# Two chunks of every feed-forward net by seven half-size products that add up in PSUM, with half-sums made by accumulating DMAs

## The chip, the cores and the metric

The kernel runs on one core of one Trainium2 chip. Times are device microseconds of one execution. The core has a matrix engine (TensorE: PE for products, PEld for its weight loads), VectorE (DVE), ScalarE (ACT), GpSimd (POOL) and SyncE (SP), which here only issues DMAs. Each engine takes its instructions in its own order; SP and POOL are also queues of DMA issues, in which an issue that has to wait holds up those behind it.

## The reference

Two layers over 256 tokens of width 1024, all in float32. Each layer is a feed-forward net, a mixer, a cross-attention to 256 memory rows and a second feed-forward net, each with a residual and a layer norm:

```python
def swiglu(x, w_gate, w_up, w_down):
    return (jax.nn.silu(x @ w_gate) * (x @ w_up)) @ w_down

for l in range(DEPTH):      # DEPTH = 2, D_MODEL = 1024, D_FF = 2816
    h = layer_norm(ALPHA * h + 0.5 * swiglu(h, ffn1_gate[l], ffn1_up[l], ffn1_down[l]), ...)
    ...                     # mixer: conv, gated recurrence, pooling; w_in, w_out
    h = layer_norm(ALPHA * h + cross_attn(h, mem, ca_q[l], ca_k[l], ca_v[l], ca_o[l]), ...)
    h = layer_norm(ALPHA * h + 0.5 * swiglu(h, ffn2_gate[l], ffn2_up[l], ffn2_down[l]), ...)
```

The four nets (`ffn1` and `ffn2` of both layers) are what the change touches, and the place of the turned memory, which `cross_attn` needs.

## The kernel before

Every float32 operand is split into two float32r parts, high and low: ACT casts the high part (L61), DVE subtracts it from the source for the low part (L62), and PE makes three products instead of one (high by high, high by low, low by high; `mm_rows`). A product of 128 x 128 by 128 x 512 is one matmul instruction (L105).

A net (`ffn`) goes over the 2816 hidden columns in chunks of 512, the last of 256. A chunk takes 2 MB of `gate` and 2 MB of `up`, in four tiles of 128 x 1024 (512 KB) each. `load` issues a tile on SP into one of 6 `raw` buffers; the split writes one of 8 `whi` and 8 `wlo` buffers, which come free when PE has used them, so ACT and DVE run at most 8 tiles ahead of PE. A plain chunk (`hidden`) is 96 matmuls: 2 token tiles x 8 rows of blocks x 3 parts x 2 matrices. Then the gated product is made on ACT (silu, L436) and DVE (L440), turned by four small DMAs and a DVE transpose (`turn`: L450, L453) and split into `ah`, `al`. `both(c, u)` takes half of a chunk through `down`: one slab of two 512 KB tiles and 24 matmuls, which add into four PSUM banks (`dn`) over the whole net. Slabs run behind the chunks: in the iteration of chunk c stand `both(c - 2, 1)` and `both(c - 1, 0)`. The last three slabs, in `end`, run row by row with the layer norm (`finish`, L332 to L358).

Some chunks go by `by_seven`: [x00 x01; x10 x11] (token halves by halves of the 1024 inputs) times [w00 w01; w10 w11] (upper and lower halves of `gate` and `up`) by seven products of 12 matmuls instead of eight, so 84 matmuls. It needs sums of blocks of x (`blocks_of_x`, made once a net from four quarters of x) and sums of weight blocks, which DVE adds in place in the raw tiles (L597): w00 + w01, then + w11, w01 + w11, then w00 + w10 by adding w10: 8 additions of 128 x 1024 per chunk. The products' results are combined on DVE (`put`, L619). Chunks 2 and 4 (the third and fifth) of three nets are done so, but in the very first net (`early` is set) chunk 4 alone: there the spare buffers hold the memory rows, which POOL loads by 32 small DMAs (L193) and DVE turns during chunk 2 (L202), and small parameters.

The order in each engine's queue is made by a scheduler from the program's dependences and its own costs; the start of the first net is written by hand (`manual_schedule` in `first`). PSUM has four `acc` banks and four `dn` banks.

Of the kernel before, what the change touches and what calls it, by code (L numbers as in the profile page):

```python
# [17 lines left out]
P = 128  # L18
# [15 lines left out]

class Weights:
# [11 lines left out]
def model(ctx: ExitStack, tc: tile.TileContext, t: dict, out: bass.AP):  # L47
# [16 lines left out]
    def load(src, k0, nk, c0, ncol, fine=False):  # L64


        hi, lo, todo = [], [], []
        step = 2048 // ncol
        for a in range(k0, k0 + nk, step):
            half = step // 2  # L70
            raw = [
                wp.tile([P, 1024], F32, tag="raw", name="raw", bufs=6).rearrange("p (k c) -> p k c", c=ncol)
                for _ in range(2)
            ]
            part = 1 if fine else half
            for b in range(0, step, part):
                loads.append(nc.sync.dma_start(
                    raw[b // half][:, b % half : b % half + part, :],
                    src[(a + b) * P : (a + b + part) * P, c0 : c0 + ncol].rearrange("(k p) c -> p k c", p=P),
                ))  # L80
# [12 lines left out]
        return Weights(hi, lo, half, todo)  # L93
# [8 lines left out]
    def product(o, w, x, start, stop):  # L102
        x = x.rearrange("p (h c) -> p c h" if len(x.shape) == 2 else "p r (h c) -> p r c h", h=2)
        o = o.rearrange("p (c h) -> p c h" if len(o.shape) == 2 else "p r (c h) -> p r c h", h=2)
        nc.tensor.matmul(o, w, x, start=start, stop=stop)  # L105
# [23 lines left out]
    def mm_rows(o, xh, xl, wh, wl, start, stop):  # L129
        product(o, xh, wh, start, False)  # L130
        product(o, xh, wl, False, False)
        product(o, xl, wh, False, stop)
# [30 lines left out]
    mT = cst.tile([P, NK, 2, SEQ], F32R, name="mT")  # L163
    xTh, xTl = xT[:, :, 0, :], xT[:, :, 1, :]
    mTh, mTl = mT[:, :, 0, :], mT[:, :, 1, :]
# [17 lines left out]
    def load_memory(mp, behind):  # L183
        m = [
            mp.tile([P, DM], F32, tag=f"spare{n}", name="m", bufs=1).rearrange("p (k b j) -> p k b j", k=4, j=32)
            for n in range(2)
# [11 lines left out]
        def later():  # L198
            for n in range(2):
                for k in range(0, 4, 2):  # L200
                    turned = mp.tile([P, 2, SEQ], F32, tag="up", name="turned")
                    nc.vector.transpose(  # L202
                        turned.rearrange("p k t -> p (k t)"), m[n][:, k : k + 2].rearrange("p k b j -> p (k b j)")
                    )
                    d = slice(4 * n + k, 4 * n + k + 2)
                    split(mTh[:, d, :], mTl[:, d, :], turned)
# [14 lines left out]
    def small_parameters(op):  # L221
        spare = op.tile([P, DM], F32, tag="spare2", name="rows", bufs=1)
# [177 lines left out]
    def ffn(l, name, n, pend=None, last=False, early=None):  # L400
        gate, up, down = (t[f"{name}_{x}"][l] for x in ("gate", "up", "down"))
        with tc.tile_pool(name="ffn", bufs=2, reuse_waits="tile") as fp:
# [24 lines left out]
            def ordered(v):  # L427
                return v.rearrange("p (a k j) -> p k a j", a=4, j=32)

            def by_two(v, o):  # L430
                o = o.rearrange("p (n a j m) -> p m n a j", n=2, a=4, m=2)
                return [(ordered(v)[:, 2 * m : 2 * m + 2], o[:, m]) for m in range(2)]

            def activate(s, i, og):
                for v, o in by_two(s[:, i, :], og):
                    nc.scalar.activation(v, o, AF.Silu)  # L436

            def gated(s, i, ou):
                for v, o in by_two(s[:, i, :], ou):
                    nc.vector.tensor_tensor(v, o, v, op=ALU.mult)  # L440
# [5 lines left out]
            def turn(s):  # L446
                ah, al = act_tiles()
                x = fp.tile([P, 4, NT, P], F32, tag="dealt", name="dealt", bufs=1)
                for a in range(4):
                    nc.sync.dma_start(x[a * 32 : a * 32 + 32], s[:, :, a * P : (a + 1) * P])  # L450
                for i in range(NT):
                    d = fp.tile([P, 4, P], F32, tag="up", name="square")
                    nc.vector.transpose(  # L453
                        d.rearrange("p k (b r) -> p b k r", b=4), x[:, :, i, :].rearrange("p b (k j) -> p b k j", k=4)
                    )
                    split(ah[:, :, tok(i)], al[:, :, tok(i)], d)
                return ah, al

            def first():
# [5 lines left out]
                if pend is None:  # L465
# [8 lines left out]
                    with tc.manual_schedule(engines={E.Activation, E.DVE, E.PE}):  # L474
# [13 lines left out]
                        def turn_x(i, j):  # L488
                            pt = acc((P, 4, P))
                            for k in range(4):  # L490
                                nc.tensor.transpose(pt[:, k, :], h[i][:, (4 * j + k) * P : (4 * j + k + 1) * P], pdn)  # L491
                            return lambda: split(
                                *(x[:, 4 * j : 4 * j + 4, tok(i)] for x in (xTh, xTl)), pt
                            )

# [56 lines left out]
            def blocks_of_x():  # L552

                for n, i, j in ((2, 0, 0), (3, 0, 1)) + (((0, 1, 0), (1, 1, 1)) if early is not None else ()):
# [13 lines left out]
            def by_seven(c0, bx):  # L568
# [19 lines left out]
                w00 = block(gate, 0, pieces("spare0", "spare1"))  # L588
                w01 = block(up, 0, pieces("lng", "lnb"))
                w11 = block(up, 1, pieces("raw", "raw"))  # L590
# [19 lines left out]
                def run(o, x, w):  # L610
                    for k in range(4):
                        wh, wl = w.at(k, slice(0, CHUNK))
                        mm_rows(o, x[0][:, k, :], x[1][:, k, :], wh, wl, k == 0, k == 3)

                def half_sum():
                    return fp.tile([P, 4, P], F32, tag="up", name="half").rearrange("p k t -> p (k t)")

                def put(o, a, op, b):
                    nc.vector.tensor_tensor(halves(o), sums(a), halves(b), op=op)  # L619

                s = activations()
                g = [s[:, i, :] for i in range(NT)]
                o = [acc((P, CHUNK)) for _ in range(4)]
                run(o[0], part_of_x(0, 0), parts_of(w00))
                nc.scalar.copy(halves(g[0]), sums(o[0]))
# [12 lines left out]
                run(o[2], part_of_x(1, 1), parts_of(w00, w10))  # L638


                def left():
                    put(e, o[0], ALU.add, e)
                    for i in range(NT):
                        put(g[i], o[1 + i], ALU.add, g[i])
                    s = fp.tile([P, NT, CHUNK], F32, tag="spare2", name="sg", bufs=1)
                    for i, u in enumerate((e, f)):
                        v = ordered(s[:, i, :])
                        nc.scalar.activation(v, g[i].rearrange("p (k a j) -> p k a j", a=4, j=32), AF.Silu)
                        nc.vector.tensor_tensor(v, v, u.rearrange("p (k a j) -> p k a j", a=4, j=32), op=ALU.mult)
# [4 lines left out]
            def last_hidden(c0):  # L654
# [3 lines left out]
                r = fp.tile([P, 2, SEQ], F32, tag="up", name="up")  # L658
# [14 lines left out]
            def slab(c, u):  # L673
                w = load(down, c * 4 + 2 * u, 2, 0, DM)
# [4 lines left out]
            sevens = (2, 4) if early is None else (4,)  # L679
# [24 lines left out]
            def aside():  # L704

                with tc.issue_after(lows[-1].ins):
                    if bx:
                        rest[1]()
                    else:
                        bx.extend(blocks_of_x())  # L710

            for c, (c0, ncol) in enumerate(chunks):
# [3 lines left out]
                elif c in sevens:  # L716
                    left = by_seven(c0, bx)
                else:
                    if c in (1, 2) and early is not None:
# [11 lines left out]
                if c == 2 and early is not None:  # L731
# [33 lines left out]
    def values(l, c, vh, vl, between={}):  # L765
        w = load(t["ca_v"][l], 0, NK, c * CHUNK, CHUNK)
        for i in range(NT):
            o = acc((P, 512))
            for k in range(NK):
# [3 lines left out]
                mm_rows(o, mTh[:, k, tok(i)], mTl[:, k, tok(i)], wh, wl, k == 0, k == NK - 1)  # L773
# [459 lines left out]
    def beginnings(op):  # L1233
        parameters, made = small_parameters(op)
        return parameters, load_memory(op, made)
# [35 lines left out]
```

## Time and profile before

| | |
|---|---|
| median of 3 runs | 1068.54 us (1068.48 to 1068.91) |
| the profiled execution | 1069.55 us, of which the span from first to last instruction is 1067.8 us |
| PE busy | 99% of the span |
| DVE, ACT busy | 89%, 61% |
| POOL busy | 6% |
| DMA packets, all 16 engines | 231.90 MB, mean 217 GB/s |
| granted TensorE clock | 0.999 |

Busy times are unions of the records of an engine. PE's matmuls are pipelined and overlap in the records, so that the time from start to start, not the length of one record, tells what a matmul takes in a row of them. In a row of a group stand line, engine, operation, what it writes and reads, the count, the busy time and the mean length in ns of one, and then the idle time of that engine just before it and what ended it. The chain of work that ended last is told from the last instruction back; a piece of it has its start, its length and its count. In a row of the stretches, each engine has its busy time and, in brackets, its number of instructions; then come the granted clock, the mean busy share of the DMA engines and GB/s.

### The profile page before, as it was taken

The numbers are of one execution on the slowest core, as the hardware profiler recorded it, in microseconds if no ns is written. First come the engines' busy times: TensorE is split into PE (matmuls) and PEld (weight loads), VectorE is DVE, ScalarE is ACT, GpSimd is POOL, SyncE is SP. The second block draws the span as 40 slices with busy tenths as digits, with TensorE's granted clock in tenths as the row PEclk, the third lists the DMA queues.
The fourth block names the chain that finished last, engine by engine and source line by source line (L and its number), as shares of the span: only waits on it lengthen the run. The fifth ranks groups of instructions, "written<-read, shape, count | busy, mean of one in ns | idle before, by whom it ended". The sixth has DMA issues, their size and how long they took to land.

```text
span 1067.8 us, 16332 instructions
## 1 busy us (share of the span) xinstructions
PE 1057.5 (99%) x5966; PEld 938.0 (88%) x5966; DVE 946.6 (89%) x1318; ACT 646.6 (61%) x922; POOL 66.9 (6%) x114
## 2 busy tenths in 40 slices
PE   9999999999999999999999999999999999999997
PEld 7888888989899888888888888888898998888886
DVE  6977997989988799999799999789899788999996
ACT  7555754767557565655575557566774665656660
POOL 9700001000000000000000000010000000000000
PEclk9999999999999999999999999999999999999999
DMA  9997494754575575847685875957536665759371
GB/s 362 261 311 254 127 287 156 260 178 159 196 271 173 174 256 192 292 161 228 226 273 180 252 261 176 295 165 232 199 114 226 238 233 175 257 157 343 127 221 40
DMA packets 130895, 231.90 MB, mean 217 GB/s; under 512 B 9408, under 2 KB 48608, under 8 KB 130816
## 3 DMA queue, kind: packets, MB, share of 16 engines
q1 hardware_dynamic: 129024, 228.49, 64.5%
q0 software_dynamic: 1216, 1.20, 0.4%
q10 hardware_dynamic: 576, 1.18, 0.3%
q8 instruction: 47, 0.77, 0.3%
q14 instruction: 32, 0.26, 0.1%
HBM read 216.15 MB, written 1.05 MB: 203 GB/s over the span
## 4 chain that ended last, share of the span: by engine, by line
PE 92%; DVE 5%; issue 1%; DMA 1%; ACT 1%; SPq 0%; DVEq 0%; ACTq 0%
PE acc L105 60%; PE dn L105 30%; DVE wlo L62 2%; PE acc L172 1%; DVE raw L597 1%; DMA dealt<-sg 1%; PE dn L955 0%; ACT whi L61 0%; DMA h<-in_x_dram 0%; PE dn L1029 0%; DVE h L358 0%; DVE sg L440 0%; PE acc L491 0%; DVE square L453 0%; DVE h L353 0%
## 5 line engine op out<-in xcount | busy, mean ns | idle before, releaser
L61 ACT CAST whi<-raw 128x1024 fp32r<-128x1024 f32 (+1 forms) x438 | 443.2, 1042 | 199.4 <-DVE raw L597 52.9
L62 DVE TENSOR_TENSOR wlo<-raw,whi 128x1024 fp32r<-128x1024 f32 (+1 forms) x438 | 516.2, 1210 | 34.3 <-ACT whi L61 30.7
L105 PE MATMUL acc<-whi,xT 128*128 128x512 f32 x1032 | 312.2, 379 | 0.0
L105 PEld LDWEIGHTS acc<-whi,xT 128*128 128x128 f32 x1032 | 195.0, 189 | 27.6
L105 PE MATMUL acc<-wlo,xT 128*128 128x512 f32 x516 | 195.7, 379 | 0.8 <-DVE wlo L62 0.8
L105 PE MATMUL acc<-xT,whi 128*128 128x512 f32 x576 | 141.0, 381 | 0.2
L105 PE MATMUL dn<-whi,ah 128*128 128x512 f32 x346 | 131.5, 380 | 0.0
L105 PE MATMUL dn<-wlo,ah 128*128 128x512 f32 x346 | 131.1, 379 | 0.0
L105 PE MATMUL dn<-whi,al 128*128 128x512 f32 x346 | 131.1, 379 | 0.0
L105 PEld LDWEIGHTS acc<-xT,whi 128*128 128x128 f32 x576 | 104.1, 190 | 12.5 <-ACT whi L61 0.7
L105 PEld LDWEIGHTS acc<-wlo,xT 128*128 128x128 f32 x516 | 97.5, 189 | 14.8 <-DVE wlo L62 1.1
L105 PE MATMUL dn<-whi,xT 128*128 128x512 f32 x288 | 87.7, 380 | 0.0
L105 PEld LDWEIGHTS acc<-xT,wlo 128*128 128x128 f32 x576 | 75.5, 191 | 3.9
L105 PE MATMUL acc<-xT,wlo 128*128 128x256 f32 x576 | 75.9, 275 | 0.0
L105 PEld LDWEIGHTS dn<-whi,al 128*128 128x128 f32 x346 | 65.4, 189 | 9.3
L105 PEld LDWEIGHTS dn<-wlo,ah 128*128 128x128 f32 x346 | 65.4, 189 | 9.2
L105 PEld LDWEIGHTS dn<-whi,ah 128*128 128x128 f32 x346 | 65.4, 189 | 9.1
L350 POOL TENSOR_TENSOR rs<-rs,nhalf 128x1 f32<-128x1 f32 x16 | 14.9, 931 | 833.6 <-DVE rs L346 599.4
L597 DVE TENSOR_TENSOR raw<-raw 128x1024 f32<-128x1024 f32 x56 | 66.1, 1216 | 0.4
L105 PEld LDWEIGHTS dn<-whi,xT 128*128 128x128 f32 x288 | 54.4, 189 | 7.5
L105 PE MATMUL dn<-wlo,xT 128*128 128x512 f32 x144 | 54.6, 379 | 0.0
L332 DVE SCALAR_TENSOR_TENSOR h<-h,dn 128x512 f32<-128x512 f32 x31 | 21.2, 685 | 30.0 <-PE dn L105 30.0
(237 smaller groups left out, 1285.5 us busy)
## 6 DMA issues: line engine op xcount, KB each, us to landing
raw<-in_ffn_up_dram SPq DMA_DIRECT2D x88, 512.0 KB, 5.4
raw<-in_ffn_down_dram SPq DMA_DIRECT2D x88, 512.0 KB, 6.5
raw<-in_ffn_gate_dram SPq DMA_DIRECT2D x84, 512.0 KB, 5.2
raw<-in_w_in_dram SPq DMA_DIRECT2D x48, 512.0 KB, 4.7
dealt<-sg SPq DMA_DIRECT2D x80, 128.0 KB, 4.3
raw<-in_ca_k_dram SPq DMA_DIRECT2D x16, 512.0 KB, 4.9
raw<-in_w_out_dram SPq DMA_DIRECT2D x16, 512.0 KB, 4.2
raw<-in_ca_v_dram SPq DMA_DIRECT2D x16, 512.0 KB, 5.0
```

The source lines that it names most:

```text
L61: nc.scalar.copy(hi, src)
L62: lows.append(nc.vector.tensor_tensor(lo, src, hi.bitcast(F32), op=ALU.subtract))
L105: nc.tensor.matmul(o, w, x, start=start, stop=stop)
L172: nc.tensor.transpose(pt[:, k, :], src[:, (4 * j + k) * P : (4 * j + k + 1) * P], unit)
L332: nc.vector.scalar_tensor_tensor(v, v, ALPHA / scale, sums(y[i][n]), op0=ALU.mult, op1=ALU.add, accum_out=None if junk is None else st[:, ...
L350: nc.gpsimd.tensor_tensor(rs, rs, nhalf[:, 0:1], op=ALU.pow)
L597: nc.vector.tensor_tensor(r[i], r[i], plus[i], op=ALU.add)
```

## The change

1. Chunks 2 and 4 of all four nets go by seven (`sevens = (2, 4)`). The built program has 5632 PE instructions in place of 5644: 12 matmuls of 128 x 512 less. Outside the four nets each engine's order is the same as before.
2. In `by_seven` the product x00 w00 stays in its PSUM bank; ACT copies it out, and three more products are added into the same bank (`more=True`), with an ACT copy in between each time. There are four `put`s and one multiplication of 128 x 1024 in place of nine smaller DVE operations, and four additions of weight blocks on DVE instead of eight.
3. The other half-sums are made by DMA: w01 + w11 and w00 + w10 by POOL's DMAs with `accum_op=ALU.add`, which read 512 KB of `up` or `gate` from HBM and add it into the raw tile. There are four of them per chunk, 32 in all. w11 is also loaded as itself.
4. Between the products stand the two slabs of chunk c - 2 (`between`). In the other iterations `both(c - 2, 0)` and `both(c - 2, 1)` follow the chunk, so the first half of each slab runs a chunk later.
5. Positions of the hidden columns: `activate` and `gated` are one instruction of 128 x 512 each in place of two of 128 x 256, `turn` makes one split of 128 x 1024 in place of two of 128 x 512, and `load(..., dealt=True)` takes every second row of `down` so that rows and columns meet. A row is 4 KB as before.
6. The memory rows and the small parameters lie where the turned memory will stand (tags `mT0`, `mT1`); they are loaded as early as before, but turned in chunk 5's iteration, just ahead of the first layer norm. The spare buffers of the first net are free for w00, whose two loads SP issues ahead of the second half of the first `up` chunk.
7. At the start of the first net ACT copies four quarters of x out of PSUM (`whole`), in place of four DVE additions later (L556).

```diff
+    early_rows, early_memory = (cst.tile([P, 2048], F32, tag=f"mT{n}", name=f"early{n}") for n in range(2))
...
+            for b in range(0, step, part):
+                to = raw[b // half][:, b % half : b % half + part, :]
+                if dealt:
+                    c, u = divmod(a // 2, 2)
+                    at = slice(c * CHUNK + 2 * P * b, c * CHUNK + 2 * P * (b + 1))
+                    rows = src[at, c0 : c0 + ncol].rearrange("(p u) c -> p u c", u=2)[:, u, :]
+                    loads.append(nc.sync.dma_start(to[:, 0, :], rows))
...
+                turned = mp.tile([P, NT, CHUNK], F32, tag="up", name="turned", bufs=1)
+                for k in range(2):
+                    nc.vector.transpose(turned[:, k, :], m[n][:, 2 * k : 2 * k + 2].rearrange("p k b j -> p (k b j)"))
+                mT.tiles[n] = cst.tile([P, 4, 2, SEQ], F32R, tag=f"mT{n}", name=f"mT{n}")
...
             def activate(s, i, og):
-                for v, o in by_two(s[:, i, :], og):
-                    nc.scalar.activation(v, o, AF.Silu)
+                nc.scalar.activation(ordered(s[:, i, :]), in_order(og), AF.Silu)
...
+                            if k < 6:
+                                nc.scalar.copy(*whole[k - 2])
...
-                o = [acc((P, CHUNK)) for _ in range(4)]
-                run(o[0], part_of_x(0, 0), parts_of(w00))
-                nc.scalar.copy(halves(g[0]), sums(o[0]))
-                run(o[2], bx[0], parts_of(w00, w01))
-                run(o[1], bx[1], parts_of(w00, w11))
-                e = half_sum()
-                put(e, o[1], ALU.add, g[0])
-                run(o[3], bx[2], parts_of(w01, w11))
-                put(g[1], o[3], ALU.add, e)
-                f = half_sum()
-                put(f, o[2], ALU.subtract, g[1])
-                put(e, o[2], ALU.subtract, e)
-                o = [acc((P, CHUNK)) for _ in range(3)]
-                run(o[0], bx[3], parts_of(w11))
-                run(o[1], part_of_x(0, 1), parts_of(w10))
-                run(o[2], part_of_x(1, 1), parts_of(w00, w10))
+                def more(to, m, j):
+                    for i in range(2):
+                        k = 4 * j + 2 * i
+                        nc.gpsimd.dma_start(
+                            to[i], m[k * P : (k + 2) * P, c0 : c0 + CHUNK].rearrange("(k p) c -> p k c", p=P),
+                            accum_op=ALU.add,
+                        )
+
+                o = [acc((P, CHUNK)) for _ in range(3)]
+                run(o[0], part_of_x(0, 0), parts_of(w00))
+                taken(s[:, 0, :], o[0])
+                run(o[1], bx[0], parts_of(w00, w01))
+                more(w01, up, 1)
+                run(o[2], part_of_x(0, 1), parts_of(w10))
+                between[0]()
+                put(s[:, 0, :], o[2], ALU.add, s[:, 0, :])
+                w11 = block(up, 1, pieces(*homes[(n + 2) % 3]))
+                run(o[0], bx[1], parts_of(w00, w11), True)
+                more(w00, gate, 1)
+                taken(e, o[0])
+                between[1]()
+                nc.scalar.activation(s[:, 0, :], s[:, 0, :], AF.Silu)
+                put(e, o[1], ALU.subtract, e)
+                run(o[0], bx[2], parts_of(w01), True)
+                taken(f, o[0])
+                o.append(acc((P, CHUNK)))
+                run(o[3], bx[3], parts_of(w11))
+                put(f, o[1], ALU.subtract, f)
+                run(o[0], part_of_x(1, 1), parts_of(w00), True)
...
-            sevens = (2, 4) if early is None else (4,)
+            sevens = (2, 4)
...
-                if c > 0:
-                    if c > 1:
-                        both(c - 2, 1)
-                    if c in sevens:
-                        acts.append(left())
-                    if c < len(chunks) - 1:
-                        both(c - 1, 0)
+                if c in sevens:
+                    acts.append(left())
+                elif c > 1:
+                    both(c - 2, 0)
+                    both(c - 2, 1)
```

More of the change, by code (lines that the diff above doesn't have):

```diff
@@ L184, in load_memory @@
         m = [
-            mp.tile([P, DM], F32, tag=f"spare{n}", name="m", bufs=1).rearrange("p (k b j) -> p k b j", k=4, j=32)
-            for n in range(2)
+            early_memory[:, n * DM : (n + 1) * DM].rearrange("p (k b j) -> p k b j", k=4, j=32) for n in range(2)
         ]
@@ L586, in block @@
                     return to
-                w00 = block(gate, 0, pieces("spare0", "spare1"))
-                w01 = block(up, 0, pieces("lng", "lnb"))
-                w11 = block(up, 1, pieces("raw", "raw"))
+                homes = [("spare0", "spare1"), ("lng", "lnb"), ("raw", "raw")]
+                n = sevens.index(c0 // CHUNK)
+                w00 = block(gate, 0, pieces(*homes[n % 3]))
+                w01 = block(up, 0, pieces(*homes[(n + 1) % 3]))
                 w10 = block(gate, 1, pieces("spare2", "raw"))
@@ L638, in by_seven @@
-                run(o[2], part_of_x(1, 1), parts_of(w00, w10))
-                def left():
[L642 to L649, printed above, removed]
+                ef = fp.tile([P, NT, CHUNK], F32, tag="up", name="halves", bufs=1)
@@ new lines, in by_seven, with taken @@
+                e, f = ef[:, 0, :], ef[:, 1, :]
+                def taken(o, bank):
+                    nc.scalar.copy(ordered(o), in_order(bank))
+                def more(to, m, j):
[5 more added lines that the diff above has]
+                        )
```

107 lines of the change are left out of this document (57 added, 50 removed).

## The prediction

> **What bounds the kernel now.** I read the page's busy shares first, then the waits of PE, the chain of work that ended last, the timeline around PE's one wait inside a net, and last the groups and stretches that say what DVE and the DMA engines can still take. First two rows of the page, then three of PE's waits (what waited, for what: us in total, times, longest), three pieces of the chain (start, length, count) and PE's timeline (start, length):
>
> ```profile
> PE 1057.5 (99%) x5966; PEld 938.0 (88%) x5966; DVE 946.6 (89%) x1318; ACT 646.6 (61%) x922; POOL 66.9 (6%) x114
> ...
> PE 92%; DVE 5%; issue 1%; DMA 1%; ACT 1%; SPq 0%; DVEq 0%; ACTq 0%
> ...
> PE dn L472 <- DVE kTh L467: 1.5, 1, 1.5
> PE acc L105 <- DVE wlo L62: 0.8, 1, 0.8
> PE acc L491 <- DMA h<-in_x_dram: 0.5, 1, 0.5
> ...
> 18.26 31.08 PE acc L105 x144
> ...
> 106.43 10.36 PE dn L105 x48
> 116.79 18.13 PE acc L105 x84
> ...
> 598.96 0.59 PE L105 MATMUL acc<-whi,xT 128*128 128x512 f32 x2
> 600.30 0.48 PE L105 MATMUL acc<-wlo,xT 128*128 128x512 f32 x1 [0.75 <-DVE wlo L62]
> 600.62 0.59 PE L105 MATMUL acc<-whi,xT 128*128 128x512 f32 x2
> ```
>
> PE is busy 99% of the span and holds 92% of the chain; inside the nets it waits once. So a change is worth the matmuls it takes off PE and the stalls that it takes or makes; work on the other engines counts only where PE comes to wait for it. The chain gives the price of a wide matmul in a row of them: 31.08 / 144 = 10.36 / 48 = 18.13 / 84 = 0.2158 us.
>
> **The matmuls.** The third chunk of the first net goes from 96 to 84: 12 x 0.2158 = 2.59 us less, all on the path. The length of a record would say otherwise:
>
> ```profile
> L61 ACT CAST whi<-raw 128x1024 fp32r<-128x1024 f32 (+1 forms) x438 | 443.2, 1042 | 199.4 <-DVE raw L597 52.9
> L62 DVE TENSOR_TENSOR wlo<-raw,whi 128x1024 fp32r<-128x1024 f32 (+1 forms) x438 | 516.2, 1210 | 34.3 <-ACT whi L61 30.7
> L105 PE MATMUL acc<-whi,xT 128*128 128x512 f32 x1032 | 312.2, 379 | 0.0
> ...
> L597 DVE TENSOR_TENSOR raw<-raw 128x1024 f32<-128x1024 f32 x56 | 66.1, 1216 | 0.4
> ...
> L625 ACT COPY sg<-acc 128x512 f32<-128x512 f32 x7 | 4.0, 578 | 0.0
> ...
> L619 DVE TENSOR_TENSOR half<-acc,sg 128x512 f32<-128x512 f32 x14 | 9.5, 681 | 0.0
> ```
>
> 12 x 379 ns = 4.55 us is not what goes, since records overlap (two matmuls last 0.59 us). [...]
>
> **The stall at 600 us.** It lies in the third chunk of the first net of layer 2, by seven. The starts there are 1.13 and 0.32 us apart over the wait, where two and one matmul need 0.43 and 0.22; with the gap ahead of it, 1.02 us are lost. Its cause is DVE. One seven with its two slabs costs DVE 18 splits x 1.21 + 8 additions x 1.216 + 9 puts x 0.68 + 2.7 for the turn = 40.3 us, while PE needs 132 x 0.2158 = 28.5 us. The 8 split buffers let DVE run ahead, but that lead is eaten in the seven. After: 18 x 1.21 + 4 x 1.216 + 4 x 0.68 + 1.2 + 2.6 = 33.2 us. The lead now shrinks by 4.7 us instead of 11.8, so I take the stall as gone: -1.02 us. If it stays, this term is 0.
>
> **PSUM reuse.** The bank that is added to must be copied by ACT (578 ns) first. With a cast ahead in ACT's queue (1042 ns) that is 1.6 us, against a shortest distance of 12 matmuls, 2.59 us; the others are 24 and 48. Hidden. Without that cover it is 1.6 us x 3 x 8 chunks.
>
> **The accumulating DMAs.** These are the unknown: 32, with no row in this trace. The nearest rows are plain loads, and POOL's memory loads, which have as many pieces. The rows below: two DMA issues of the page (KB each, us to landing); the memory tile `m`; the landing of `raw` in 28–50, 410–433 and 433–464 us; and three stretches.
>
> ```profile
> raw<-in_ffn_up_dram SPq DMA_DIRECT2D x88, 512.0 KB, 5.4
> ...
> raw<-in_ffn_gate_dram SPq DMA_DIRECT2D x84, 512.0 KB, 5.2
> ...
> L193 POOL DMA_DIRECT2D m<-in_mem_dram x32: 584/584/637, 27.8 to 49.5; - x32
> ...
> DMA to landing us min/median/max: 4.2/8.1/9.5
> DMA to landing us min/median/max: 3.5/4.3/5.3
> DMA to landing us min/median/max: 3.5/6.0/7.8
> 8.00:49.00 41.00, 41.00 (x192) 35.87 (x191) 37.90 (x48) 29.48 (x42) 36.77 (x61) 1.00 1.02 323
> 410.00:433.00 23.00, 23.00 (x108) 20.12 (x107) 23.00 (x27) 13.46 (x15) 0.00 (x0) 1.00 0.53 161
> 433.00:464.00 31.00, 31.00 (x145) 27.14 (x145) 29.00 (x31) 19.37 (x25) 0.00 (x0) 1.00 0.93 322
> ```
>
> An add reads its destination as well, so I bound a landing by one plain load, 5.2 us, below, and by twice the longest landing of the crowded start, 2 x 9.5 = 19.0 us, above. I take 2 x 5.2 = 10.4 us: the sevens lie in stretches with landings of 4.3 us and a DMA share of 0.53, nearer to the plain 5.2 than to the start. What is needed: in the built order the tightest pair (the halves of w00 + w10) has 8.2 to 11.2 us of matmuls between POOL's issue and ACT's cast. A late cast stalls not PE at once but ACT's queue: behind it stands the copy out of the shared bank, which PE adds to 24 matmuls (5.2 us) after that run's end. So PE stalls when a landing takes over some 14.3 us (66 matmuls). At 10.4 the cost is 0. [...] POOL's issues cost 0.58 us each on an engine that has no other work in the sevens. Their 16.8 MB (32 x 512 KB) come onto the 231.90 MB of all packets, and a share of 0.53 leaves room.
>
> **Loads and slabs.** SP's queue keeps 546 issues: loads of w11 as itself take the place of those of the addends that POOL now reads. Splits on DVE go from 430 of full width to 436, ACT's instructions from 867 to 886: 6 x 1.21 us against 24 additions less. Half-slabs that run a chunk later and stand between the products add no matmul: 0, and they lengthen the time that ACT and DVE have inside a seven; that was counted above as 132 matmuls.
>
> **Gating, turn, memory.**
>
> ```profile
> 66.33 1.30 DVE L202 STREAM_TRANSPOSE turned<-m 128x512 f32<-128x512 f32 x2
> ...
> 164.86 0.69 DVE L332 SCALAR_TENSOR_TENSOR h<-h,dn 128x512 f32<-128x512 f32 x1 [1.17 <-PE dn L105]
> ...
> 168.75 0.69 DVE L332 SCALAR_TENSOR_TENSOR h<-h,dn 128x512 f32<-128x512 f32 x1 [3.19 <-PE dn L105]
> ...
> 10.06 2.18 ACT L61 CAST whi<-raw 128x512 fp32r<-128x512 f32 x4
> 12.78 1.05 ACT L61 CAST whi<-raw 128x1024 fp32r<-128x1024 f32 x1 [0.53 <-DMA raw<-in_ffn_up_dram]
> ```
>
> Joined instructions for gating and split replace pairs of the same width: 0. The turned memory costs DVE 4 x 0.65 and 4 x 0.64 = 5.2 us, moved from 66 us to just ahead of the layer norm at 162 us. There DVE idles 1.17 and 3.19 us, and PE has 24 matmuls (5.2 us) more of slabs ahead of the tail: 9.6 us against 5.2, so 0; uncovered it would be up to 5.2. At the start ACT gets four copies of 578 ns, 2.3 us, in 10–14 us. The first cast of `up` behind them waits 0.53 us for its DMA anyway, and PE needs `up` only at 18.26: 0. SP issues three tiles of 512 KB for the first seven ahead of the rest of `up`. The loads set the pace there:
>
> ```profile
> 15.26 1.06 ACT L61 CAST whi<-raw 128x1024 fp32r<-128x1024 f32 x1 [0.21 <-DMA raw<-in_ffn_up_dram]
> 16.53 1.04 ACT L61 CAST whi<-raw 128x1024 fp32r<-128x1024 f32 x1 [0.21 <-DMA raw<-in_ffn_up_dram]
> ```
>
> A tile lands each 1.27 us, so the last two of `up`, cast at 15.26 and 16.53, come 3.8 us later, at 19.1 and 20.4. PE takes a tile in 12 matmuls, 2.59 us, and `up` from 18.26 on, so it needs the third and fourth from 23.4 and 26.0: 0. The same shift reaches w01 of the first seven, the last tile to be loaded for it. I estimate its landing at 43 to 49 us (the start's loads at 1.27 us a tile, and the 1 MB of memory among them), and PE's order needs it from about 48. That is between 0 and 2.6 us (12 matmuls, the run that waits); I take 0, as most of that span lies ahead of 48.
>
> **Sum.** -2.59 - 1.02 = -3.6 us. The profiled execution took 1069.55 us (its span 1067.8), so 1065.9; it stood 1.0 us above the median 1068.54, so the median goes to 1064.9. A difference of 0.2%, 2.1 us, is about what a measurement here tells from none.
>
> **Rivals.**
> 1. Small stalls eat part of it: w01 late at 48 us (2.6), or the tail's 5.2 us of memory work half exposed. For it: the DMA share is 1.02 in 8–49 us, and w00 comes on top. Against: only one of the four nets is loaded so. 1066.4 to 1067.5, no measurable change.
> 2. The accumulations land late. From 14.3 us on, each further us costs 8 us, one for each chunk by seven; at 14.75 the gain is gone. At twice the crowded median, 16.2 us: 1.9 x 8 = +15 us, some 1080; at 19.0: +38, some 1102. For it: 7.8 and 9.5 us do occur, with DMA shares of 0.93 and 1.02, and 433–464 follows right behind a seven. Against: most loads in the sevens themselves take 4.3.
> 3. POOL's DMAs start only when DVE is idle. DVE is busy 23.00 of 23.00 us in 410–433. If each had to wait some 18 us there, 18 + 5.2 - 14.3 = 8.9 us x 8 = +71, some 1136. Against: POOL issued its memory loads in 584 to 637 ns each with DVE busy 37.90 of 41.00 us. [...]
> 4. The change brings its matmuls but not the stall: DVE still lags at one seven, as 33.2 us remain above PE's 28.5. 1065.9, still faster.
>
> **How the numbers follow.** The forecast with rival 4, 0.66: the matmuls are certain, and the terms behind them small. Rival 1, 0.11. Rival 2, 0.20, since its price is without a row and its edge only 1.4 times the value taken. Rival 3, 0.03. So faster 0.66, same 0.11, slower 0.23. The range goes from 1063.8 (another 1.1 us out of the 10.3 in which PE isn't busy) over rival 1 into rival 2 up to 1080, its middle price; above that some 0.13 are left out. The forecast's own range is 1063.8 to 1066.
>
> **What would show it.** Right: wide matmuls still 0.216 us apart, 12 fewer; no wait of PE for `wlo` near 600 us; POOL's `raw` landing below 14 us; DVE's additions 32 x 1.2 us, its busy time 40 us or more lower. Wrong: PE waiting in all eight sevens, with ACT's `whi` released by POOL's DMA (rival 2), or those DMAs starting long after their issue (rival 3); or a wait of PE at 48 us or at the first layer norm (rival 1).

## The result, and the profile after

The changed kernel takes 1072.48 us (median; 1070.08 to 1077.51) where the kernel before takes 1068.66 us beside it (1068.45 to 1069.7): ratio 1.0035, 95% interval 1.0021 to 1.0049. It was forecast at 1064.9 us. The profiled execution took 1071.74 us, its span 1069.9, so it stands 0.7 us below its median. Four rows of the page of the changed kernel (busy shares; two DMA issues with KB each and median us to landing), the landing of all 32 accumulating DMAs, four waits of PE (us in total, times, longest) and the groups that the prediction had costed:

```profile
PE 1057.8 (99%) x5954; PEld 937.3 (88%) x5954; DVE 913.4 (85%) x1225; ACT 658.4 (62%) x903; POOL 102.0 (10%) x146
...
raw<-in_ffn_up_dram POOLq DMA_DIRECT2D x16, 512.0 KB, 6.3
raw<-in_ffn_gate_dram POOLq DMA_DIRECT2D x16, 512.0 KB, 9.3
...
DMA to landing us min/median/max: 5.8/8.3/12.7
...
PE acc L126 <- ACT sg L652: 2.1, 1, 2.1
PE dn L492 <- DVE kTh L487: 1.5, 1, 1.5
PE acc L511 <- DMA h<-in_x_dram: 0.4, 1, 0.4
PE acc L126 <- ACT halves L652: 0.2, 1, 0.2
...
L623 DVE TENSOR_TENSOR raw<-raw 128x1024 f32<-128x1024 f32 x32 | 38.8, 1221 | 0.8 <-DMA raw<-in_ffn_up_dram 0.4
L657 POOL DMA_DIRECT2D raw<-in_ffn_up_dram x16 | 19.3, 1232 | 248.5 <-DMA raw<-in_ffn_down_dram 111.8 <-DMA dealt<-sg 70.8 <-DMA raw<-in_ffn_up_dram 35.9
```

PE has its 12 instructions less, DVE is busy 33 us less, the accumulating DMAs land within 12.7 us, and the wait for `wlo` at 600 us is not there. There is one new wait of size: 2.1 us for an ACT copy (L652, `taken`), and a small one for another such copy (`halves`). The first stands in the first seven of the first net. PE's timeline there, and the stretches of the wait, of the slow matmuls behind it and of a seven elsewhere, where the DMA share was 0.53 before (busy time and count of PE, PEld, DVE, ACT, POOL; granted clock; DMA share; GB/s):

```profile
62.55 0.38 PE L126 MATMUL dn<-whi,al 128*128 128x512 f32 x1
65.03 0.48 PE L126 MATMUL acc<-whi,kTh 128*128 128x512 f32 x1 [2.10 <-ACT sg L652]
65.35 0.38 PE L126 MATMUL acc<-wlo,kTh 128*128 128x512 f32 x1
...
66.86 0.63 PE L126 MATMUL acc<-whi,kTh 128*128 128x512 f32 x1
67.28 0.63 PE L126 MATMUL acc<-wlo,kTh 128*128 128x512 f32 x1
67.71 0.63 PE L126 MATMUL acc<-whi,kTl 128*128 128x512 f32 x1
...
62.40:65.00 2.60, 0.53 (x3) 0.12 (x1) 2.60 (x3) 2.60 (x5) 1.05 (x1) 1.00 1.11 270
65.00:69.40 4.40, 4.37 (x12) 3.52 (x13) 4.40 (x7) 2.57 (x4) 0.00 (x0) 0.61 1.11 242
410.00:433.00 23.00, 23.00 (x108) 20.14 (x107) 21.29 (x22) 15.62 (x18) 2.38 (x2) 1.00 1.04 255
```

The stall costs twice. From 62.55 to 65.03 are 2.48 us where 0.22 were due, and then eight matmuls start 0.427 us apart, with the granted clock at 0.61 in that stretch (0.50 from 66 to 68 us): 4.0 us together. Against a second profiled execution of the kernel before (1068.75 us, below) the account is: 12 matmuls -2.6, this stall +4.0, the layer norm of the first net +0.7, the wait for `halves` at 605 us +0.5, a start that is 0.3 later: +2.9 of 3.0 us.

The wait for `halves` has an accumulating DMA behind it. Two pieces of the chain of work, with start, length and count, then a row of ACT and one of PE:

```profile
588.96 12.69 DMA raw<-in_ffn_gate_dram
602.62 2.94 ACT whi L75 x3
...
605.47 0.57 ACT L652 COPY halves<-acc 128x512 f32<-128x512 f32 x1
...
606.09 0.48 PE L126 MATMUL acc<-whi,xT 128*128 128x512 f32 x1 [0.23 <-ACT halves L652]
```

The DMA lands at 601.65; the cast that waits for it and three more stand on ACT ahead of the copy.

What held the copy at 62 us is on ACT and DVE. Their timelines before the wait:

```profile
53.92 1.05 ACT L75 CAST whi<-raw 128x1024 fp32r<-128x1024 f32 x1 [0.98 <-PE acc L126]
59.66 4.84 ACT L75 CAST whi<-raw 128x1024 fp32r<-128x1024 f32 x5 [4.68 <-DVE raw L623]
64.40 0.57 ACT L652 COPY sg<-acc 128x512 f32<-128x512 f32 x1
...
53.73 0.68 DVE L458 TENSOR_TENSOR sg<-acc,sg 128x512 f32<-128x512 f32 x1
54.33 1.22 DVE L76 TENSOR_TENSOR wlo<-raw,whi 128x1024 fp32r<-128x1024 f32 x1
55.46 0.68 DVE L458 TENSOR_TENSOR sg<-acc,sg 128x512 f32<-128x512 f32 x1
56.06 2.35 DVE L76 TENSOR_TENSOR wlo<-raw,whi 128x1024 fp32r<-128x1024 f32 x2
58.33 1.22 DVE L623 TENSOR_TENSOR raw<-raw 128x1024 f32<-128x1024 f32 x1
```

The copy of x00 w00, whose product had long been done, stands on ACT behind five casts, and the first of these waits 4.68 us for DVE's addition of w11 at 58.33. The copy also waits for a buffer: it writes `sg`, which the four turning DMAs of the chunk before still read, and those come behind the gating (L458), which DVE did only at 53.73 and 55.46. By the chain of waits they landed at 64.02. Both ways lead to DVE, which was busy without a gap from 44.5 to 59.6 us.

### The profile page after: what moved, and what is told of

Same layout as the page of the kernel before. It is cut to its first block, busy times and chain, and to the rows that moved or that the text cites. A ratio compares the mean times of both kernels' runs of the same rounds, so it can differ in the third digit from the quotient of the medians.

```text
span 1069.9 us, 16330 instructions
## 1 busy us (share of the span) xinstructions
PE 1057.8 (99%) x5954; PEld 937.3 (88%) x5954; DVE 913.4 (85%) x1225; ACT 658.4 (62%) x903; POOL 102.0 (10%) x146
## 4 chain that ended last, share of the span: by engine, by line
PE 88%; DVE 4%; DMA 3%; ACT 2%; issue 1%; SPq 0%; DVEq 0%; ACTq 0%
PE acc L126 59%; PE dn L126 26%; DMA raw<-in_ffn_gate_dram 2%; DVE wlo L76 2%; PE acc L193 1%; ACT whi L75 1%; DVE raw L623 1%; DMA dealt<-sg 1%; DMA raw<-in_ffn_up_dram 1%; PE dn L993 0%; SPq L468 0%; DVE sg L458 0%; PE dn L1067 0%; DMA h<-in_x_dram 0%; PE acc L511 0%
## 5 line engine op out<-in xcount | busy, mean ns | idle before, releaser
L76 DVE TENSOR_TENSOR wlo<-raw,whi 128x1024 fp32r<-128x1024 f32 (+1 forms) x444 | 525.1, 1210 | 62.3 <-ACT whi L75 48.0
L75 ACT CAST whi<-raw 128x1024 fp32r<-128x1024 f32 (+1 forms) x444 | 448.9, 1042 | 198.9 <-PE dn L126 60.1
L126 PE MATMUL acc<-whi,xT 128*128 128x512 f32 x992 | 300.7, 380 | 0.2 <-ACT halves L652 0.2
L126 PEld LDWEIGHTS acc<-whi,xT 128*128 128x128 f32 x992 | 187.5, 189 | 27.1 <-ACT halves L652 0.6
L126 PE MATMUL acc<-wlo,xT 128*128 128x512 f32 x496 | 188.0, 379 | 0.0
L126 PEld LDWEIGHTS acc<-wlo,xT 128*128 128x128 f32 x496 | 93.8, 189 | 13.2
L126 PEld LDWEIGHTS acc<-xT,wlo 128*128 128x128 f32 x576 | 75.5, 191 | 3.9
L126 PE MATMUL acc<-whi,kTh 128*128 128x512 f32 x128 | 49.2, 384 | 2.1 <-ACT sg L652 2.1
L126 PE MATMUL acc<-wlo,kTh 128*128 128x512 f32 x128 | 49.3, 385 | 0.0
```

Of the source, the lines that this page charges most:

```text
L75: nc.scalar.copy(hi, src)
L76: lows.append(nc.vector.tensor_tensor(lo, src, hi.bitcast(F32), op=ALU.subtract))
L126: nc.tensor.matmul(o, w, x, start=start, stop=stop, skip_group_check=more)
```

## The experiments

All times are medians, with the ratio to the kernel before measured beside them, and its 95% interval. The theory after the result (A): DVE has no lead over PE left at the first seven of the first net. The rival (B): the accumulating DMAs cost something in every seven.

**One seven in the first net.**

```diff
-            sevens = (2, 4)
+            sevens = (2, 4) if early is None else (4,)
```

> In the first net only chunk 4 goes by seven, as in the kernel before; every other part of the change stays. Theory A (the loss is one stall of PE in the first seven of the first net, at 62 us, with the slow matmuls behind it): 12 matmuls come back (+2.59 us) and the stall of 2.3 + 1.7 us and its spread go, so about 1070 us or less, 1069 to 1070.5, and repeated runs lie within 1 us of each other. Theory B (the accumulating DMAs cost something in all eight sevens): seven of eight sevens stay, so 1071.5 to 1075, with the spread of the changed kernel.

1068.94 us, 1.0006 (0.9996 to 1.0015), runs between 1068.73 and 1070.07. PE waits for no split and no copy in any of the seven sevens left. So the loss sits in that one place, and B falls for the other seven sevens. But it also says that the rest of the change brings nothing: this kernel has the matmuls of the kernel before, and its time.

**A buffer of its own for the copy.**

```diff
-                taken(s[:, 0, :], o[0])
+                x00 = s[:, 0, :]
+                if early is not None and n == 0:
+                    x00 = sm.tile([P, 2, SEQ], F32, tag="sums", name="sums", bufs=1).rearrange("p a b -> p (a b)")
+                taken(x00, o[0])
...
-                put(s[:, 0, :], o[2], ALU.add, s[:, 0, :])
+                put(s[:, 0, :], o[2], ALU.add, x00)
```

> In the first seven of the first net the copy of the product x00 w00 goes to a buffer of its own and no longer waits for the four turning DMAs that still read `sg`; the scheduler then puts it five casts earlier on ACT, nothing else moves. Theory A1 (the copy is late, by the wait for `sg` and the casts ahead of it): PE's wait of 2.1 us at 62 us and the slow matmuls go, about 4 us, 1067.5 to 1069. Theory A2 (DVE and the casts are late anyway, the copy only happened to be last): PE waits at the next place within the same seven, for a split, and 2 us or more of the stall stay, 1070 to 1072. Theory B: no change, 1071.5 to 1073.

1070.08 us, 1.0014 (1.0004 to 1.0023). The copy now runs at 54.68, and PE waits for the next two copies instead (its waits, then two rows of ACT):

```profile
PE acc L126 <- ACT halves L652: 2.5, 2, 1.4
...
73.69 3.88 ACT L75 CAST whi<-raw 128x1024 fp32r<-128x1024 f32 x4 [2.22 <-DMA raw<-in_ffn_gate_dram]
...
77.48 0.57 ACT L652 COPY halves<-acc 128x512 f32<-128x512 f32 x1
```

The time is A2's, at its lower edge, though A2 expected a wait for a split: the copy was the first of several late things. The last of them, at 77.5 us, stood behind four casts, of which the first waited for the accumulating DMA of w00 + w10. POOL issued that at 62.05 us, and it landed 11.6 us later. This is the path of rival 2 of the prediction, in this one chunk, with a landing below its limit of 14.3 us.

**Without the sums of x, and with more DVE work.** The first leaves out four sums of the first net, the second adds four operations.

```diff
-                    nc.vector.tensor_tensor(q[o], q[a], q[b], op=op)
+                    if early is None:
+                        nc.vector.tensor_tensor(q[o], q[a], q[b], op=op)
```

```diff
                     split(*parts[n], q[o])
+                    if early is not None:
+                        nc.vector.tensor_tensor(q[o], q[o], q[o], op=ALU.max)
```

> Left out in the first net: the four sums and differences of quarters of x (4 x 0.60 us of DVE at 30 to 38 us), so the two chunks by seven of that net get other operands. Theory A2 (DVE is behind at the start of the first net): everything that DVE does up to 62 us comes 2.4 us earlier, the gating and with it the turning DMAs too, so the wait of 2.1 us shrinks to 0 to 0.3 and no slow matmuls follow: 1067.5 to 1069. If instead the loads set the pace there (DMA share 1.04): the wait stays above 1.5 us, 1071 to 1073.

> Four more DVE operations of the same kind (the maximum of a quarter sum with itself) in the first net, 4 x 0.60 us at 30 to 40 us: the suspected load is raised by as much as the run without the sums lowers it. Theory A2: the wait at 62 us grows from 2.1 to about 4.5 us, with slow matmuls behind it for about as long as before, 1074 to 1076. If the loads set the pace: 1071 to 1073.

Without the sums 1071.78 us, 1.0036 (1.002 to 1.0052): no better, against A2's expectation. With more work 1073.01 us, 1.0043 (1.0028 to 1.0058), above the changed kernel by less than expected. By the two expectations these times lie where loads that set the pace would put them, or at its edge. One row of PE's timeline without the sums, and two of PE's waits with more work:

```profile
57.38 0.77 PE L126 MATMUL acc<-whi,xT 128*128 128x512 f32 x1 [2.87 <-DVE sg L458]
```

```profile
PE acc L126 <- ACT sg L654: 2.5, 1, 2.5
PE acc L126 <- DVE sg L458: 1.6, 1, 1.6
```

But neither is a clean test: the scheduler wrote another order on DVE, ACT and (without the sums) SP. In both, PE waits for the gating of chunk 1 itself, since the product's bank is free only after it. Without the sums DVE had four splits and two additions ahead of the gating and did it at 56.55 to 57.8, later than before, with less to do. That turned the question from how much DVE does to what stands first in its queue.

**The gating first.** The splits of w10 may not be issued on DVE ahead of the gating; once with the copy's own buffer, once alone.

```diff
+                gates.append(nc.vector.tensor_tensor(v, in_order(ou), v, op=ALU.mult))
...
-                run(o[2], part_of_x(0, 1), parts_of(w10))
+                with tc.issue_after(gates[-1].ins) if early is not None and n == 0 else nullcontext():
+                    w = parts_of(w10)
+                run(o[2], part_of_x(0, 1), w)
```

> In the first seven of the first net: the gating of the chunk before it stands ahead of the splits of w10 on DVE (in the changed kernel it comes behind splits and additions, at 53.7 and 55.5 us), and the copy of x00 w00 has a buffer of its own, as in the run with the own copy. Both sums stay as they are. Theory A (DVE has lost its lead there, and what stands first in its queue decides who is late): gating at about 49 us, the turn some 4 us earlier, so the second copy, which waits for the turn's buffer, is in time; PE waits under 1 us in this seven, 1066.5 to 1068.5, and if so faster than the kernel before. If there is simply too much DVE work for any order: the wait moves to a split in the same seven, 1069 to 1071.

> The changed kernel with one edit: in the first seven of the first net the gating of the chunk before it stands ahead of the splits of w10 on DVE. The copy of x00 w00 stays where it writes `sg`. If the gating that came late on DVE is the cause: the turn and with it the copy come some 4 us earlier, PE's wait at 62 us goes, 1068 to 1069.5, as with both edits. If it takes the buffer of its own as well: a wait of 1 us or more of PE for the copy stays, 1069.5 to 1072.

With both 1068.87 us, 1.0004 (0.9995 to 1.0013); alone 1068.67 us, 1.0002 (0.9993 to 1.0011). A change of order alone takes the wait at 62 us away. DVE and ACT of the run with the gating first, one of its waits, and its stretch from 49 to 66 us:

```profile
50.37 2.36 DVE L623 TENSOR_TENSOR raw<-raw 128x1024 f32<-128x1024 f32 x2
52.64 1.28 DVE L458 TENSOR_TENSOR sg<-acc,sg 128x512 f32<-128x512 f32 x2
...
51.00 4.83 ACT L75 CAST whi<-raw 128x1024 fp32r<-128x1024 f32 x5
60.42 0.59 ACT L652 COPY sg<-acc 128x512 f32<-128x512 f32 x1 [4.60 <-DMA dealt<-sg]
...
PE acc L126 <- ACT halves L652: 0.6, 1, 0.6
...
49.00:66.00 17.00, 17.00 (x79) 14.60 (x78) 16.42 (x18) 10.30 (x13) 4.88 (x4) 1.00 1.07 252
```

The last gating comes 2.2 us earlier and, since the scheduler also drew the additions of w11 forward, the last of these some 7 us earlier. ACT has no late cast in front of the copy, which now waits for the turn alone and is done before PE needs it. Since the scheduler moved the gating, the additions, ACT's casts and some of SP's loads together, the runs don't tell which of these moves it was. The DMA share is 1.07 from 49 to 66 us, as in the changed kernel, so the crowded DMA engines alone don't make the wait.

In this profiled execution the first layer norm is reached 1.1 us ahead of the second profiled execution of the kernel before, with 1.5 us of waits left over: -2.6 less 1.5, so the matmuls are worth what they were counted at. The larger part of these waits, 0.8 us at 75.5, is again a copy behind four casts, the first of which waits for the accumulating DMA of w00 + w10 (issued at 61.0 us, landed 11.0 later). With both edits PE also waits for a split in this seven, where under 1 us of waits was expected:

```profile
PE acc L126 <- DVE wlo L76: 1.1, 1, 1.1
```

So DVE's lead is used up there in either order.

**The place in the net.** Chunks 3 and 4 by seven in the first net; then also the small parameters in chunk 2.

```diff
-            sevens = (2, 4)
+            sevens = (2, 4) if early is None else (3, 4)
```

```diff
-                if c == 3 and early is not None:
+                if c == 2 and early is not None:
                     with tc.issue_after(lows[-1].ins):
                         rest[0]()
+                if c == 3 and early is not None:
                     turn_memory = load_memory(fp, loads[-1])
```

> In the first net chunks 3 and 4 go by seven, one right behind the other, instead of 2 and 4: as many matmuls as the changed kernel. Theory A (the lead of DVE over PE, 8.5 us at the first seven of this net against 13 to 15 at the others, is what is missing): at chunk 3 the lead is back at some 14 us, so that seven runs without a wait; the one behind it starts with some 5 us and may wait 0 to 2 us: 1066.3 to 1069. If the first net is bad for a second seven wherever it stands (loads, memory rows): 1070 to 1073.

> As the run with chunks 3 and 4 by seven in the first net, but the work on the small parameters (a dozen short DVE operations, an exponential and two table loads on ACT, at 102 to 126 us between the two chunks by seven) goes to chunk 2, which is a plain one there. Theory A (DVE's lead decides): the second of the two chunks keeps 2 to 4 us more of its lead and PE's wait of 0.7 us at 126 us and the one of 0.7 at 102 us go: 1066.3 to 1067.8, faster than the kernel before. If the waits there come from the loads: no change, about 1068.

1068.12 us, 0.9996 (0.9987 to 1.0006), and 1068.49 us, 0.9996 (0.9987 to 1.0005). Chunk 3 by seven runs with one wait of 0.3 us in the first of the two runs and none in the second, so a second seven is not bad for this net as such. In the first run PE waits 0.7 us for a split at 126 us, in the second seven; with the parameters moved that is 0.2, but 1.5 us come up at the layer norm, where DVE's `h` is late, so the 1066.3 to 1067.8 us that were expected of it did not come. These are the best times of the study, and neither is told apart from the kernel before.

The lead can be read from the trace, as the time from the end of a split on DVE to the first matmul that takes it, with splits and tiles paired in order. In the changed kernel it is 8.5 us at the start of the first net's first seven and falls to 1.8 in it; at the seven at 412 us it is 15.0 for the first tile, 7.7 for the second, and falls to 5.0. At the same 50 us the kernel before had 8.7 to 11, with a plain chunk ahead.

**What the accumulating DMAs bring, and when they are late.** Both on the kernel with one seven in the first net: plain loads and DVE additions in their place; and each of them twice.

```diff
-                        nc.gpsimd.dma_start(
-                            to[i], m[k * P : (k + 2) * P, ...], accum_op=ALU.add,
-                        )
+                        r = pieces("raw")[0]
+                        loads.append(nc.sync.dma_start(r, m[k * P : (k + 2) * P, ...]))
+                        nc.vector.tensor_tensor(to[i], to[i], r, op=ALU.add)
```

```diff
-                    for i in range(2):
+                    for i in (0, 1, 0, 1):
```

> As the run with one seven in the first net, but the half-sums by plain loads on SP and four more DVE additions per chunk in place of the accumulating DMAs: 28 additions of 1.2 us more. Theory A: the accumulating DMAs are hidden, and what they save is DVE's lead in a seven (4.9 us of some 5 left at its end); so short waits of PE come back at the ends of some sevens, 0 to 1 us each: 1069 to 1073. Theory B (the accumulating DMAs cost time): faster than with them, under 1068.5.

> As the run with one seven in the first net, but each accumulating DMA is issued twice, the second behind the landing of the first, so that the operand holds the addend twice and comes about twice as late: 2 x 8.4, for `gate` 2 x 9.3 us. By the prediction's limit of 14.3 us PE waits about 2 to 5 us in each of the seven chunks: 1083 to 1105. If the limit is wider than 19 us: 1069 to 1071.

With DVE's additions 1068.76 us, 1.0003 (0.9994 to 1.0013), and no wait of PE in a net at all: the 28 operations that the DMAs spare cost nothing, where short waits and 1069 to 1073 us were expected. Twice: 1150.31 us in one execution, beyond every expectation. Waits of PE and a piece of ACT at 440 us with them doubled:

```profile
PE acc L126 <- ACT halves L652: 33.5, 10, 8.5
PE acc L126 <- ACT sg L652: 23.6, 3, 9.1
...
439.57 1.04 ACT L75 CAST whi<-raw 128x1024 fp32r<-128x1024 f32 x1 [7.63 <-DMA raw<-in_ffn_up_dram]
440.53 0.58 ACT L652 COPY sg<-acc 128x512 f32<-128x512 f32 x1
```

So the mechanism of rival 2 is real: a late landing holds a cast, the cast holds the copy behind it, the copy holds PE. The size exceeds the expectation: PE waits 57 us for copies, where 14 to 35 were expected. POOL's queue stood still for 143.9 us in all ahead of the 28 second issues, and the granted clock of this execution was 0.972, where it was 0.998 in the profiled one with the DMAs issued once.

**Memory rows later.** POOL's 32 loads behind the first seven's accumulating DMAs, in the changed kernel and in the one with the gating first.

```diff
-                        nc.gpsimd.dma_start(
+                        adds.append(nc.gpsimd.dma_start(
...
-                    turn_memory = load_memory(fp, loads[-1])
+                    turn_memory = load_memory(fp, adds[3])
```

> The changed kernel with only the memory loads behind the accumulating DMAs of the first seven; no other engine's order changes. If the crowded DMA engines are a cause of their own of the wait at 62 us: the loads up to 50 us land earlier, the turning DMAs take 4 to 5 us instead of 5.8, and the wait of 2.1 us falls below 1, 1068 to 1069.5. If it is the order on DVE alone: the gating stays at 53.7 and 55.5 us and the wait at 1.5 to 2.5 us, 1071 to 1073.

> The kernel with the gating first, and POOL's 32 loads of memory rows (1 MB, in the changed kernel at 28 to 48 us) behind the accumulating DMAs of the first seven; no other engine's order changes. The DMA share is 1.05 to 1.07 at 30 to 66 us. If this crowding, together with the late gating, is what makes the first seven late: the rest of the waits (0.9 us at 75 us) and the spread of the runs (1068.0 to 1071.3) go, median 1066.5 to 1067.8, faster than the kernel before. If the crowding does not matter: 1068.3 to 1069, with the spread as it was.

In the changed kernel 1070.9 us, 1.002 (1.0011 to 1.003), with the wait as it was:

```profile
PE acc L126 <- ACT sg L652: 2.3, 1, 2.3
...
59.46 4.84 ACT L75 CAST whi<-raw 128x1024 fp32r<-128x1024 f32 x5 [4.69 <-DVE raw L623]
64.20 0.57 ACT L652 COPY sg<-acc 128x512 f32<-128x512 f32 x1
```

The gating stayed at 53.5 and 55.3 us, the casts at 59.5. So the memory loads are not the cause. The median is 1.6 us lower, but the intervals of the two ratios overlap. At 49 to 66 us the DMA share stayed at 1.07, so this run did not take that crowding away. With the gating first, the later memory rows made it worse: 1070.92 us, 1.0019 (1.0011 to 1.0028), with waits of 1.0 us for a split at 120 us and 2.0 us at the layer norm.

**The kernel before once more.**

> The kernel before once more, for its trace. The prediction took the wait of PE for DVE at 600 us (1.02 us with the gaps around it) to be there in the median run. If it is: the wait shows again. If it was an accident of the one profiled execution, whose time stood 1.0 us above the median: no wait of PE for a split, and a time near 1068.6.

1068.75 us in one execution, and these are all of PE's waits:

```profile
PE dn L472 <- DVE kTh L467: 1.5, 1, 1.5
PE acc L491 <- DMA h<-in_x_dram: 0.6, 1, 0.6
```

The stall at 600 us is not there. From the first layer norm to 543 us the two executions stay within 0.4 us of each other, and from 600 us on this one is 0.8 us ahead. Of the 98 runs of the kernel before that were measured beside the others, 29 took 1069.0 us or more, as the first profiled execution did; whether these have the stall, no trace shows.

## Why the prediction was wrong

Of the 7.6 us between the forecast and the median, the profiled execution shows 6.5: the stall at 62 us (4.0), the stall at 600 us that the median run did not have (1.0), the layer norm (0.7), the wait at 605 us (0.5) and the later start (0.3). Some 0.7 more is its distance from its own median.

- **The matmuls, -2.59 us: right.** The spacing is 0.216 us still, and where the stall is gone the first net is shorter by 2.6 us less the waits that are left.
- **The stall at 600 us, -1.02 us: wrong.** It was taken for a property of the kernel, but the second profiled execution does not have it. The sign stood in the prediction: that execution took 1.01 us more than the median, and the sum takes this microsecond off twice, as the stall and as the step down to the median. Against the median there was nothing to gain; -2.59 alone gives some 1066. The same goes for DVE's relief, 33 us where 40 or more were expected: it is real, and it was worth nothing, since PE did not wait for DVE.
- **PSUM reuse, 0: the step that failed, by 4.0 us.** It put one cast ahead of ACT's copy, 1.6 us against the shortest distance of 2.59, and took the distances of 24 and 48 matmuls as safe. The stall came at the longest: 48 matmuls, 10.4 us, lie between the product x00 w00 and the next use of its bank, and the copy was done 12.6 us behind the product. In the built order five casts stand ahead of this copy and are bound to a DVE addition, and the copy has a second wait, for the buffer that the turn still reads, which the step did not name. In the sevens elsewhere PE does not wait for this copy, and DVE's lead is at least 3.4 us there, against 1.8 here; that the lead is what hides it there is argued from this, not shown by itself. The sum of 33.2 us against 28.5 asked only how fast the lead shrinks over a whole seven (4.7 us), not how much of it there is at 49 us nor how deep it falls on the way: 6.7 us here, 10 at 412 us. Why it is only 8.5 us at 49 us stays open; loads that pace the start are one reason that no run here tests.
- **The lower clock behind the stall: not foreseen.** Eight matmuls start 0.427 us apart instead of 0.216, at a granted clock of 0.50 from 66 to 68 us. It is 1.7 of the 4.0 us.
- **The accumulating DMAs, 0: right to 0.5 us, with a limit that was too wide.** 6.3 and 9.3 us by source, where 10.4, an estimate of twice a plain load, was taken within 5.2 to 19.0, and no landing passed 14.3. But the one of 12.7 us at 589 us cost 0.5, and with other orders one of 11.6 and one of 11.0 in the first seven cost 1.3 and 0.8: three more casts, 2.9 us, stand between the cast that waits and the copy, and the prediction did not name them. The DMA share at 410 to 433 us did not stay at 0.53 either; it is 1.04. POOL's issue took 1.2 us, twice the 0.58 assumed, and cost nothing. Rival 2 did not happen as told, in all sevens. The doubled DMAs show that its mechanism is real; they do not test its price of 8 us for each us.
- **Start, loads, memory: nearly right.** DVE waited 0.41 us for `up` (w01) at 44.5 us and PE did not wait there: rival 1's place was wrong, 48 us, though its net was right. The turned memory, taken as 0, stands in the chain ahead of the layer norm, where some 0.7 us are lost. ACT has 19 instructions less (x903 after x922), where the working has 19 more; nothing hung on it.
- **Rivals and chances.** The slower side had 0.23, all of it for DMAs in all sevens. The case that came, one late seven that costs more than the 12 matmuls bring, stood in rival 1 as a loss that ends within 0.2%. That 1072.48 us lies inside the range all the same is luck: the range reaches there only to take in rival 2 at 1080.

What stays open: why the runs of the changed kernel spread over 7 us and those of the best orders over 3, where the kernel with one seven in that net spreads over 1.3. The mean granted clock is 0.998 in the shortest run of the changed kernel and 0.995 in the longest, which points to more time at a lower clock in the long runs. The thin places lie in the first net, but only a profiled execution shows them, and of these kernels there is one of each.

## What to carry to other kernels

Before a chunk is made dearer for the engines that feed PE, read how far they are ahead of PE at that very place: 8.5 us at 50 us was not enough, in the order that the scheduler wrote, for what 12 to 16 us carry elsewhere, and the same edit one chunk later ran with a wait of 0.3 us at most. When an in-order engine makes a copy that PE needs, count all that stands ahead of it in the built order and what each of those waits for, and every buffer that the copy writes. Take a wait of one profiled execution as a gain only if that execution's time is the median's.

## What was not expected of the hardware

A short stall can be followed by a lower clock: behind the one of 2.48 us, which ended at 65.03 us, the granted clock was 0.61 for 4.4 us (0.50 from 66 to 68 us), and 1.00 again from 69.4 us on. Without the sums of x, behind a gap of 3.25 us from start to start that ended at 57.38 us, matmuls start 0.43 us apart too. Behind 1.13 us at 600 us in the first profiled execution of the kernel before, and behind 1.08 us at 126 us with chunks 3 and 4 by seven, they are 0.216 us apart from the second on. Over all profiled executions, from 9 us on, thirteen gaps of 0.9 to 2.0 us were followed by matmuls at 0.216 us throughout; of ten gaps from 2.2 to 3.3 us five were followed by 5 to 8 matmuls 0.427 us apart and five by none; all seven from 4.7 to 9.5 us by 8 to 13.

An accumulating DMA of 512 KB landed after 8.3 us in the median (5.8 to 12.7) beside medians of 5.2 to 6.0 for plain loads of `up` and `gate` in the two kernels: 1.4 to 1.6 times, less than the twofold that the prediction took.
